# An 8-byte tile made 1024 bytes wide, in a two-layer transformer kernel in split float32

## The chip, the cores and the metric

The kernel runs on one core of one Trainium2 chip. The metric is the device time of one execution in microseconds (us); with one core it is that core's time. The inputs lie in HBM, all 16 of them in float32.

## The reference

Two layers on 256 tokens of width 2048. The first is a stick-breaking attention, the second a sparse attention in three branches (compressed, selected, window); each is followed by an MLP with a squared ReLU. Cut to what the change lies in:

```python
D_MODEL, SEQ, D_FF = 2048, 256, 8192
def sqrelu_mlp(h, w1, w2):
    return jnp.square(jax.nn.relu(h @ w1)) @ w2
...
for layer in range(2):
    if layer == 0: h = h + stick_breaking_attention(rms_norm(h, sb_norm_g[0]), ...)
    else:          h = h + native_sparse_attention(rms_norm(h, nsa_norm_g[0]), ...)
    h = h + sqrelu_mlp(rms_norm(h, mlp_norm_g[layer]), mlp_w1[layer], mlp_w2[layer])
```

## The kernel before

Each weight is read from HBM once and split into two numbers of the chip's rounded float32 type: hi = rounded(w), written by ScalarE (ACT) at line 142, and lo = w - hi, written by VectorE (DVE) at line 144. The activations are split as well (xhi and xlo in one tile xs; yhi and ylo). A product is three matmuls: hi with hi, hi with lo, lo with hi.

The unit of work is a chunk: 512 KB of weights (256 rows by 512 columns, or 512 by 256), loaded by a DMA of the SP queue into one of five buffers `raw`; in the MLPs every sixth load goes into `raw6` instead. Four hi and four lo buffers follow. TensorE (PE) uses a chunk in one of three ways:

- `chunk_T` (matmuls at line 206, 24 of them, 256 columns each): the weights are the stationary operand, the activations xs the moving one. It makes the transposed product, for `h @ w1`.
- `chunk_N` (line 173, 12 matmuls of 512 columns): the activations are stationary, the weights move, for the products with `w2` and others.
- `chunk_S` (line 269, 21 matmuls of 256 columns): the same product in the manner of Strassen, with 7 block products in place of 8. Four of the seven need sums of weight blocks, which DVE writes into a tile `ts` and which are split into hi and lo; the other three use weight blocks as they are, split into tiles `shi` and `slo`. The stationary operands are parts of yhi and ylo and of `ss`, sums of activation blocks.

`mlp` works through the 8192 hidden columns in four pieces (fg 0 to 3). For each, `group1` makes 2048 hidden columns in four blocks of 8 chunk_T; from the second piece on, a chunk_S for the previous piece's product is put in after the third and the sixth chunk_T of every block. `group2` then multiplies by `w2`: 16 chunk_N (24 in the last piece), with 8 chunk_S put between them. Per MLP that makes 24 chunk_S in group1 and 32 in group2. The order is that in which the code is written; each engine runs its instructions in that order and waits on semaphores.

Where tiles lie. The pools are laid out one behind the other, each tile of a pool behind the one before it in blocks of 32 bytes, and the code shifts some operands on purpose. The names used below: P is 128, `far` and the offsets `FAR` move a tile's start by 16 floats, 64 bytes.

```python
PAD, FAR = 64, 16
def far(pool, n, name, dtype=F32R, bufs=1):
    return pool.tile([P, n + PAD], dtype, name=name, bufs=bufs)[:, FAR:FAR + n]
...
o = (FAR, FAR) if ahi is yhi else (0, 0)          # chunk_N: where hi and lo begin in their buffers
hi, lo = ... load_split(..., o=o, gap=PAD - FAR if turn else 0)
...
W = NB // 2                                        # chunk_S
hi, lo = [wsum.tile([P, 3 * W], F32R, tag=n, name=n, bufs=1) for n in ("shi", "slo")]
```

With `turn`, the second half of a chunk's lo begins 192 bytes further on than it else would. `mlp` sets it for each chunk_N that stands before a chunk_S, and for a piece's last chunk_N. In the built program, a row of SBUF being counted in bytes from its partition's start, the operands' starts are these, modulo 256:

| operand | before | after |
|---|---|---|
| xs (moving at line 206) | 128 | 128 |
| hi, lo as weights of line 206 | 192 | 192 |
| hi, lo moving at line 173 in the MLPs | 192 | 192 |
| second half of a turned lo there | 128 | 128 |
| yhi, ylo, ss as weights of lines 173 and 269 | 192 | 192 |
| hi, lo of the sums, moving at line 269 | 128 | 128 |
| shi, slo, moving at line 269 | 160 | 128 |
| raw6, pre, uv, sq, sums, ts (ACT, DVE and DMA only) | 160 | 128 |
| raw | 128 | 128 |

Of the kernel before, what the change touches and what calls it, by code (L numbers as in the profile page):

```python
# [8 lines left out]
F32 = mybir.dt.float32  # L9
# [6 lines left out]
P = 128  # L16
T = 256
NT = T // P
# [23 lines left out]
def hybrid_kernel(  # L42
# [23 lines left out]
    def far(pool, n, name, dtype=F32R, bufs=1):  # L66
        return pool.tile([P, n + PAD], dtype, name=name, bufs=bufs)[:, FAR:FAR + n]
# [97 lines left out]
    def bank(pool, tag):  # L165
        return pool.tile([P, NB], F32, tag=tag, name=tag)
# [49 lines left out]
    def proj_T(ps, src, n0, nk=KC, then={}):  # L216

        for i in range(KD // nk):
            k0 = i * nk
            chunk_T(ps, src, k0, n0, k0 == 0, k0 + nk == KD, nk)  # L220
            if i in then:
                then[i]()
# [57 lines left out]
    def banks_S(pool, tag):  # L280

        W = NB // 2
        bs = [bank(pool, tag) for _ in range(4)]
        half = lambda j, i: bs[j][:, i * W:(i + 1) * W]
        return bs, [half(0, 0), half(1, 0), half(1, 1), half(2, 0), half(2, 1), half(3, 1), half(3, 0)]

    def add_S(nb, bs, ps, pool, scale):

        W = NB // 2
        uv = pool.tile([P, 4, W], F32, tag="pre", name="uv", bufs=1)  # L290
        u, v = uv[:, :2, :], uv[:, 2:, :]
        hb = [h[:, t, nb * NB:(nb + 1) * NB] for t in range(NT)]
        nc.scalar.activation(u[:, 0, :], ps[0], AF.Copy)
        nc.vector.tensor_tensor(v[:, 0, :], ps[5], u[:, 0, :], op=OP.add)
        nc.vector.tensor_tensor(u[:, 1, :], ps[4], v[:, 0, :], op=OP.add)
        nc.vector.tensor_tensor(v[:, 1, :], ps[6], v[:, 0, :], op=OP.add)
        f0, f1 = scale[:, 0:1], scale[:, 1:2]
        add = lambda o, x, f: nc.vector.scalar_tensor_tensor(o, x, f, o, op0=OP.mult, op1=OP.add)
        add(hb[0], bs[1], f0)
        add(hb[1], bs[2], f1)  # L300
        add(hb[0], u.rearrange("p a n -> p (a n)"), f0)
        add(hb[1].rearrange("p (a n) -> p a n", a=2), v[:, 1, :].unsqueeze(1).to_broadcast([P, 2, W]), f1)
# [8 lines left out]
    def split_evac(hi, lo, src, scale=None):  # L311

        if scale is None:
            nc.scalar.activation(hi, src, AF.Copy)  # L314
            nc.vector.tensor_tensor(lo, src, hi.bitcast(F32), op=OP.subtract)  # L315
        else:
            nc.scalar.activation(hi, src, AF.Copy, scale=scale)
            nc.vector.scalar_tensor_tensor(
                lo, src, scale, hi.bitcast(F32), op0=OP.mult, op1=OP.subtract
            )  # L320
# [44 lines left out]
    def make_rstd(layer):  # L365
        s = small.tile([P, NT], F32, tag="ms", name="ms")
        nc.vector.tensor_reduce(s, ssq_t[layer], axis=AX.X, op=OP.add)
        nc.vector.tensor_scalar(s, s, 1.0 / D, EPS, op0=OP.mult, op1=OP.add)
        r = small.tile([P, NT], F32, tag="rstd", name="rstd")
        nc.gpsimd.tensor_tensor(r, s, neghalf[:, :NT], op=OP.pow)  # L370
        return r
# [8 lines left out]
    def add_h(nb, ps, scale=None):  # L380
        for t in range(NT):
            hb = h[:, t, nb * NB:(nb + 1) * NB]
            if scale is None:
                nc.vector.tensor_tensor(hb, ps[t], hb, op=OP.add)
            else:
                nc.vector.scalar_tensor_tensor(hb, ps[t], scale[:, t:t + 1], hb, op0=OP.mult, op1=OP.add)

    def add_out(nb, ps, ov, scale):

        for t in range(NT):  # L390
            for i in range(2):
                w = NB // 2
                c = slice(nb * NB + i * w, nb * NB + (i + 1) * w)
                nc.vector.scalar_tensor_tensor(
                    h[:, t, c], ps[t][:, i * w:(i + 1) * w], scale[:, t:t + 1], h[:, t, c], op0=OP.mult, op1=OP.add
                )
                (nc.sync, nc.scalar)[i].dma_start(ov[:, t, c], h[:, t, c])
# [19 lines left out]
    def mlp(l, layer, junk, done, last=None):  # L417
        w1, w2 = mlp_w1[l], mlp_w2[l]
        ss = far(junk, KD * 4 * P, "ss").rearrange("p (a k i n) -> p a k i n", a=2, k=KD // 2, i=4)
        factor = junk.tile([P, NT], F32, name="factor", bufs=1)  # L420

        def factors():
            yield
            r = make_rstd(layer)
            nc.vector.tensor_tensor(factor, r, r, op=OP.mult)

        def in_S(fg, nb):

            for i in range(NK):
                if i == 0:  # L430
                    bs, s = banks_S(att, "att")
                chunk_S(s, w2, fg * KD + i * KC, nb * NB, i == 0, i == NK - 1, yhi, ylo, ss[:, 0], ss[:, 1],
                        koff=fg * KD)
                if i == NK - 1:
                    add_S(nb, bs, s, junk, factor)
                yield

        def group1(fg, beside_w1):

            step = lambda: next(beside_w1)  # L440
            for fb in range(D // NB):
                ps = [bank(acc, "acc") for _ in range(NB // P // 2)]
                proj_T(ps, w1, fg * D + fb * NB, then={2: step, 5: step} if beside_w1 else {})
                k, n = fb * (NB // P), NB // P
                a = junk.tile([P, n, T], F32, tag="pre", name="pre", bufs=1)
                for j in range(0, n, 2):
                    nc.scalar.activation(a[:, j:j + 2, :], ps[j // 2].rearrange("p (m t) -> p m t", m=2), AF.Relu)
                s = junk.tile([P, n, T], F32, tag="sq", name="sq", bufs=1)
                nc.scalar.activation(s, a, AF.Square)
                nc.scalar.activation(yhi[:, k:k + n, :], s, AF.Copy)  # L450
                nc.vector.tensor_tensor(ylo[:, k:k + n, :], s, yhi[:, k:k + n, :].bitcast(F32), op=OP.subtract)

                sv = s.rearrange("p (j kk) t -> p j kk t", kk=2)
                a1, a2 = [[sv[:, :, kk, t * P:(t + 1) * P] for kk in (1, 0)] for t in range(NT)]
                q = junk.tile([P, 2, 4, P], F32, tag="sums", name="sums", bufs=1)
                nc.vector.scalar_tensor_tensor(q[:, :, 0, :], a2[0], -1.0, a2[1], op0=OP.mult, op1=OP.subtract)
                nc.vector.tensor_tensor(q[:, :, 2, :], a1[0], a2[0], op=OP.subtract)
                nc.vector.tensor_tensor(q[:, :, 1, :], a2[1], q[:, :, 2, :], op=OP.subtract)
                nc.vector.tensor_tensor(q[:, :, 3, :], a1[1], q[:, :, 1, :], op=OP.subtract)
                split_evac(ss[:, 0, k // 2:k // 2 + 2], ss[:, 1, k // 2:k // 2 + 2], q)  # L460

        def group2(fg, end):

            blocks = (0, 1, 3) if end else (0, 1)
            side, si = in_S(fg, 2), 0
            for j in range(len(blocks) * NK):
                nb, i = blocks[j // NK], j % NK
                if i == 0:
                    ps = [bank(acc, "acc") for _ in range(NT)]
                out = last is not None and end and nb == 3  # L470
                aside = si < NK and j >= 4 + (1.75 if end else 1.4) * si
                chunk_N(ps, w2, fg * KD + i * KC, nb * NB, i == 0, i == NK - (2 if out else 1), yhi, ylo,
                        koff=fg * KD, by_token=out and i == NK - 1,
                        turn=aside or (not end and j == len(blocks) * NK - 1))
                if i == NK - 1:
                    if out:
                        add_out(nb, ps, last, factor)
                        return
                    add_h(nb, ps, factor)
                    if end and nb == 3:  # L480
                        done(nb, (att, "att"))
                if aside:
                    next(side)
                    si += 1
                    if si == NK and end:
                        for n in range(3):
                            done(n, (att, "att"))

        spawn(factors(), 1)
        NK = KD // KC  # L490
        for fg in range(DFF // D):
            group1(fg, in_S(fg - 1, 3) if fg else None)
            group2(fg, fg == DFF // D - 1)


    with tc.tile_pool(name="sbp", bufs=2) as sp:
# [77 lines left out]
        factor = []  # L574
# [547 lines left out]
```

## Time and profile before

| | |
|---|---|
| median of 3 runs | 2173.13 us (2172.14 to 2173.88) |
| profiled execution, its time | 2172.32 us |
| its span, first to last instruction | 2170.6 us |
| PE busy, matmuls | 2163.3 us, 14894 instructions |
| DVE busy | 1569.7 us |
| ACT busy | 1235.9 us |
| read from HBM | 401.83 MB, 186 GB/s over the span |
| MLP of layer 0, of layer 1 | about 400 to 1070 us, about 1482 us to the end |

In rows of the profile L206 is line 206 of the kernel; `acc<-xs,hi` says what an instruction writes and reads; x696 is a count. In the chain of work that ended last, a piece is a start (us from the span's start), a duration and what ran. In a window's row each engine has its busy time and its count, then come the granted TensorE clock, the share of the DMA engines and GB/s. In a row of a group the numbers behind the count are the busy time in us and the mean of one in ns, and behind the bar the idle time before it with what ended it.

### The profile page before, as it was taken

The numbers are of one execution on the slowest core, as the hardware profiler recorded it, in microseconds if no ns is written. First come the engines' busy times: TensorE is split into PE (matmuls) and PEld (weight loads), VectorE is DVE, ScalarE is ACT, GpSimd is POOL, SyncE is SP. The second block draws the span as 40 slices with busy tenths as digits, with TensorE's granted clock in tenths as the row PEclk, the third lists the DMA queues.
The fourth block names the chain that finished last, engine by engine and source line by source line (L and its number), as shares of the span: only waits on it lengthen the run. The fifth ranks groups of instructions, "written<-read, shape, count | busy, mean of one in ns | idle before, by whom it ended". The sixth has DMA issues, their size and how long they took to land.

```text
span 2170.6 us, 37272 instructions
## 1 busy us (share of the span) xinstructions
PE 2163.3 (100%) x14894; PEld 2000.6 (92%) x14894; DVE 1569.7 (72%) x2131; ACT 1235.9 (57%) x1653; POOL 45.2 (2%) x75
## 2 busy tenths in 40 slices
PE   9999999999999999999999999999999999999999
PEld 9999988998998999999898888889989989989998
DVE  5555555567778778778776887755777787787786
ACT  6555565565555555555555666655555555555553
POOL 0000000000000000000000011000000000000000
PEclk9999999999999999999999999999999999999999
DMA  7655556665656665665667554456566556656664
GB/s 243 206 164 182 168 169 192 187 198 183 208 185 201 197 191 183 208 195 185 193 186 217 165 146 141 141 177 191 185 197 211 176 194 204 194 184 204 193 193 148
DMA packets 260789, 406.34 MB, mean 187 GB/s; under 512 B 13188, under 2 KB 91912, under 8 KB 260616
## 3 DMA queue, kind: packets, MB, share of 16 engines
q1 hardware_dynamic: 259800, 403.52, 59.9%
q8 instruction: 116, 1.90, 0.3%
q14 instruction: 57, 0.47, 0.1%
q10 hardware_dynamic: 816, 0.46, 0.1%
HBM read 401.83 MB, written 2.10 MB: 186 GB/s over the span
## 4 chain that ended last, share of the span: by engine, by line
PE 98%; DVE 1%; DMA 0%; ACT 0%; issue 0%; POOL 0%; SPq 0%; DVEq 0%; ACTq 0%; POOLq 0%
PE acc L206 43%; PE acc L173 36%; PE att L269 13%; PE att L173 1%; PE att L944 1%; PE att L328 1%; DMA raw<-in_nsa_w_in_dram 0%; DVE lo L144 0%; PE att L655 0%; PE att L607 0%; PE att L882 0%; PE att L938 0%; PE att L884 0%; PE att L883 0%; PE att L936 0%; PE att L937 0%
## 5 line engine op out<-in xcount | busy, mean ns | idle before, releaser
L142 ACT ACTIVATE hi<-raw 128x1024 fp32r<-128x1024 f32 x639 | 676.4, 1060 | 616.7 <-PE acc L206 320.4
L144 DVE TENSOR_TENSOR lo<-raw,hi 128x1024 fp32r<-128x1024 f32 x639 | 777.7, 1222 | 294.4 <-ACT hi L142 282.9
L206 PE MATMUL acc<-xs,hi 128*128 128x256 f32 x5360 | 677.5, 279 | 0.0
L206 PEld LDWEIGHTS acc<-xs,hi 128*128 128x128 f32 x5360 | 646.0, 188 | 1.0
L206 PE MATMUL acc<-xs,lo 128*128 128x256 f32 x2680 | 365.4, 279 | 0.0
L206 PEld LDWEIGHTS acc<-xs,lo 128*128 128x128 f32 x2680 | 335.1, 189 | 0.0
L173 PE MATMUL acc<-hi,yhi 128*128 128x512 f32 x828 | 324.0, 391 | 0.0
L173 PE MATMUL acc<-hi,ylo 128*128 128x512 f32 x828 | 322.6, 390 | 0.0
L173 PE MATMUL acc<-lo,yhi 128*128 128x512 f32 x828 | 224.2, 392 | 0.0
L142 ACT ACTIVATE hi<-ts 128x1024 fp32r<-128x1024 f32 x112 | 118.9, 1061 | 141.0 <-PE acc L173 82.3
L173 PEld LDWEIGHTS acc<-lo,yhi 128*128 128x128 f32 x828 | 154.6, 188 | 31.7
L173 PEld LDWEIGHTS acc<-hi,ylo 128*128 128x128 f32 x828 | 155.5, 188 | 29.3 <-DVE ylo L315 0.2
L173 PEld LDWEIGHTS acc<-hi,yhi 128*128 128x128 f32 x828 | 155.5, 188 | 29.0 <-ACT yhi L314 0.2
L173 PE MATMUL acc<-hi,xs 128*128 128x512 f32 x704 | 177.2, 392 | 0.0
L245 DVE TENSOR_TENSOR ts<-raw 128x512 f32<-128x512 f32 x112 | 77.4, 691 | 131.2 <-DMA raw<-in_mlp_w_dram 130.9
L173 PEld LDWEIGHTS acc<-hi,xs 128*128 128x128 f32 x704 | 130.2, 188 | 26.3
L144 DVE TENSOR_TENSOR lo<-ts,hi 128x1024 fp32r<-128x1024 f32 x112 | 136.5, 1219 | 5.7 <-ACT hi L142 5.7
L247 ACT ACTIVATE shi<-raw 128x768 fp32r<-128x768 f32 x112 | 95.0, 848 | 55.9 <-PE att L269 39.5
L250 DVE TENSOR_TENSOR slo<-raw,shi 128x768 fp32r<-128x768 f32 x112 | 106.9, 954 | 16.6 <-PE att L269 16.4
L269 PE MATMUL att<-hi,ss 128*128 128x256 f32 x672 | 97.3, 281 | 0.0
L173 PE MATMUL acc<-lo,xs 128*128 128x512 f32 x352 | 97.1, 396 | 0.0
L269 PEld LDWEIGHTS att<-hi,ss 128*128 128x128 f32 x672 | 86.6, 188 | 0.0
(248 smaller groups left out, 2128.3 us busy)
## 6 DMA issues: line engine op xcount, KB each, us to landing
raw<-in_mlp_w_dram SPq DMA_DIRECT2D x512, 512.0 KB, 4.2
raw<-in_sb_w_qkv_dram SPq DMA_DIRECT2D x95, 512.0 KB, 3.9
raw<-in_nsa_w_in_dram SPq DMA_DIRECT2D x50, 512.0 KB, 3.7
raw<-in_sb_w_out_dram SPq DMA_DIRECT2D x32, 512.0 KB, 3.8
raw<-in_nsa_w_in_dram SPq DMA_DIRECT2D x64, 256.0 KB, 4.0
raw<-in_nsa_w_out_dram SPq DMA_DIRECT2D x32, 512.0 KB, 3.6
w1t<-in_nsa_cmp_w_dram SPq DMA_DIRECT2D x8, 512.0 KB, 4.1
h<-in_x_dram SPq DMA_DIRECT2D x8, 256.0 KB, 4.7
```

What stands on the lines that cost most here:

```text
L142: nc.scalar.activation(hi, raw, AF.Copy)
L144: nc.vector.tensor_tensor(lo, raw, hi.bitcast(F32), op=OP.subtract)
L173: mm = lambda a, b, k, t, s, e: nc.tensor.matmul(ps[t], a[:, k, t * P:(t + 1) * P], b, start=s, stop=e)
L206: nc.tensor.matmul(o, w, x[:, k0 + kk, :], start=s, stop=e, skip_group_check=True)
L245: nc.vector.tensor_tensor(ts[:, :2, :], flat[:, W:3 * W].rearrange("p (a n) -> p a n", a=2), b12, op=OP.subtract)
L247: nc.scalar.activation(hi, flat[:, :3 * W], AF.Copy)
L250: nc.vector.tensor_tensor(lo, flat[:, :3 * W], hi.bitcast(F32), op=OP.subtract)
L269: nc.tensor.matmul(ps[i], a, w, start=s, stop=e, skip_group_check=True)
L328: nc.tensor.transpose(ps[:, j * T + t * P:j * T + (t + 1) * P], h[:, t, (kp + j) * P:(kp + j + 1) * P], ident)
L944: nc.tensor.transpose(ptp[:w, j * P:(j + 1) * P], src(j), ident)
```

## The change

The tile `factor` (two floats for each partition: the square of the norm's factor for the two token tiles) is allocated with 256 floats, of which the first two are used. It is the second tile of the MLPs' pool, behind `ss`. Before, it took 32 bytes in each partition, after, 1024; all tiles of the pool behind it begin 992 bytes later. Nothing else differs: each engine has the same instructions in the same order.

```diff
         ss = far(junk, KD * 4 * P, "ss").rearrange("p (a k i n) -> p a k i n", a=2, k=KD // 2, i=4)
-        factor = junk.tile([P, NT], F32, name="factor", bufs=1)
+        factor = junk.tile([P, T], F32, name="factor", bufs=1)[:, :NT]
```

## The prediction

> **What bounds the kernel now.** I read the page first, then the waits of TensorE (PE), then the chain of work that ended last piece by piece, then windows over single lines, and at a few boundaries the timeline.
>
> ```profile
> span 2170.6 us, 37272 instructions
> PE 2163.3 (100%) x14894; PEld 2000.6 (92%) x14894; DVE 1569.7 (72%) x2131; ACT 1235.9 (57%) x1653; POOL 45.2 (2%) x75
> PEclk9999999999999999999999999999999999999999
> ```
> ```profile
> PE att L515 <- POOL ident masks.py:199: 1.6, 1, 1.6
> PE acc L534 <- ACT hi L527: 0.8, 1, 0.8
> PE att L789 <- DVE hs L784: 0.5, 1, 0.5
> PE att L836 <- DVE kc L831: 0.4, 1, 0.4
> ```
>
> PE is busy all the time at the full granted clock, and these four are all of its listed waits: 3.3 us, none of them in an MLP. So no DMA, ACT or DVE row of the MLPs is worth anything by itself; the kernel gets faster only if PE's own stream of matmuls runs denser. "Busy" does not tell how dense it is, because matmuls overlap. The pace, the time from one matmul's start to the next one's, has to be taken from the chain, whose pieces give a duration and a count. In the chain's longest pieces and around the first MLP's second group:
>
> ```profile
> 357.40 16.38 PE acc L173 x72
> 400.58 78.90 PE acc L206 x696
> 564.58 14.13 PE acc L206 x120
> 1472.47 5.66 PE acc L206 x48
> 1478.56 2.74 PE acc L206 x24
> 1481.74 78.90 PE acc L206 x696
> 1099.95 27.33 PE acc L206 x232
> ...
> 711.22 2.48 PE att L269 x21
> 716.43 8.17 PE acc L206 x72
> 724.61 2.48 PE att L269 x21
> 727.08 8.48 PE acc L206 x72
> 738.04 14.13 PE acc L206 x120
> ```
>
> The reader is to see two paces of one and the same instruction, the 128x256 matmul of line 206. Piece 400.58: 78.90/696 = 113.4 ns. Piece 564.58: 14.13/120 = 117.8 ns. In the second half of the list the switch is caught in the act: three chunks of line 206 run 8.17/72 = 113.5 ns, then comes one chunk of line 269 (the Strassen-like chunk_S), and the next three run 8.48/72 = 117.8 ns, and so on to the group's end. The chunk_S itself runs 2.48/21 = 118.1 ns. It is no matter of the clock, and no wait stands between:
>
> ```profile
> 440.00:470.00 30.00, 30.00 (x267) 30.00 (x266) 1.00 0.63 196
> 593.00:605.00 12.00, 12.00 (x104) 12.00 (x104) 1.00 0.58 197
> ```
>
> Both windows over line 206 show PE busy throughout and clock 1.00, the first before any chunk_S, the second between two of them.
>
> So the pace is something that the stream keeps until it is tipped over. What tips it over I read by laying the addresses of the built program beside the trace. At line 206 the moving operand (xs) begins at 128 modulo 256 and the weights at 192, at both paces. In chunk_S the weights (yhi, ylo, ss) are at 192 too, the moving hi and lo at 128, but the moving shi and slo at 160. Nine of its 21 matmuls stand at that other distance, and the fast stream does not come back after the first of them. Twice more the trace shows that a foreign distance sets the pace: piece 1472.47 comes straight from 128x512 matmuls with moving operand and weights both at 192 and runs slow (5.66/48 = 117.9), until four transposes end it (1478.56 reads 114 ns, 1481.74 is fast); piece 1099.95 follows two transposes with weights at 64 and is slow for all its 232 matmuls.
>
> **The change, part by part.** No instruction is added, removed or moved: each engine's order is the same. What changes is where nine tiles lie, raw6, pre, uv, sq, sums, both ts, shi and slo: from 160 to 128 modulo 256.
>
> *ACT, DVE.* Their cost at the two places can be read now, since raw lies at 128 and ts at 160:
>
> ```profile
> L142 ACT ACTIVATE hi<-raw 128x1024 fp32r<-128x1024 f32 x639 | 676.4, 1060 | 616.7 <-PE acc L206 320.4
> L144 DVE TENSOR_TENSOR lo<-raw,hi 128x1024 fp32r<-128x1024 f32 x639 | 777.7, 1222 | 294.4 <-ACT hi L142 282.9
> L142 ACT ACTIVATE hi<-ts 128x1024 fp32r<-128x1024 f32 x112 | 118.9, 1061 | 141.0 <-PE acc L173 82.3
> L144 DVE TENSOR_TENSOR lo<-ts,hi 128x1024 fp32r<-128x1024 f32 x112 | 136.5, 1219 | 5.7 <-ACT hi L142 5.7
> ```
>
> 1060 against 1061 ns and 1222 against 1219: nothing. *DMA.* One load in six goes to raw6. The trace has it under raw's name, so its landing can't be told apart; it lies behind ACT, which idles 320 us for PE at line 142, that is, the loads run ahead. I take zero for it; were it dearer or cheaper, the same cover would hide it.
>
> *PE in group1.* After the change all 21 matmuls of chunk_S have the distance of line 206 (moving 128, weights 192). I take it that the quick pace then goes on through chunk_S and behind it, as it goes on through 696 matmuls at 400.58 that change weights, banks and moving tile all the time. chunk_S: 2.48 - 21 x 0.1134 = 0.10 us, and group1 has 8 of them in 3 of 4 groups of 2 layers: 48 x 0.10 = 4.8 us. Line 206 behind them: of a group's 32 chunks the first three are fast already, 29 chunks x 24 matmuls x 6 groups = 4176 x (117.8 - 113.4 = 4.4 ns) = 18.4 us. Bounds for this term: 0 if the pace doesn't hold, 18.4 if it does everywhere; I take the upper one, since of the rows above every stretch that keeps the distance keeps its pace.
>
> *PE in group2.* Here chunk_S stands between chunks of line 173, moving and weights both at 192. Going in and coming out in the quick pace have their own prices, which two boundaries show:
>
> ```profile
> 715.35 1.08 PE L173 MATMUL acc<-lo,yhi 128*128 128x512 f32 x4
> 716.27 1.99 PE L206 MATMUL acc<-xs,hi 128*128 128x256 f32 x16
> 718.10 1.07 PE L206 MATMUL acc<-xs,lo 128*128 128x256 f32 x8
> 719.00 1.98 PE L206 MATMUL acc<-xs,hi 128*128 128x256 f32 x16
> 720.82 1.07 PE L206 MATMUL acc<-xs,lo 128*128 128x256 f32 x8
> ...
> 1560.47 0.39 PE L173 MATMUL acc<-hi,yhi 128*128 128x512 f32 x1
> 1560.71 0.40 PE L173 MATMUL acc<-hi,ylo 128*128 128x512 f32 x1
> 1560.94 0.39 PE L173 MATMUL acc<-hi,yhi 128*128 128x512 f32 x1
> 1561.17 0.39 PE L173 MATMUL acc<-hi,ylo 128*128 128x512 f32 x1
> ```
>
> At 715.35 a "turned" chunk, whose last two matmuls read lo at 128, precedes line 206: the first sixteen take 716.27 to 718.10 = 1.83 us, the later sixteen 719.00 to 720.82 = 1.82. In: 0.01 us. The same turn stands before every chunk_S of group2. At 1560.47 the fast line 206 is left for 192: the first three steps take 0.70 us, 0.233 each, where 16.38/72 = 0.2275 is usual. Out: 0.02 us. Left over: 0.10 - 0.03 = 0.07 us x 64 chunks = 4.5 us. Bounds: 0 and 6.4 (no price in or out).
>
> *Given back.* Six groups now end fast and pay 0.02 each: 0.1 us. DVE has to keep up:
>
> ```profile
> 826.00:887.00 61.00, 61.00 (x353) 53.88 (x351) 51.49 (x68) 35.11 (x37) 0.00 (x0) 1.00 0.59 188
> 887.00:998.00 111.00, 111.00 (x936) 110.52 (x935) 83.36 (x102) 61.31 (x66) 0.00 (x0) 1.00 0.64 199
> GB/s 243 206 164 182 168 169 192 187 198 183 208 185 201 197 191 183 208 195 185 193 186 217 165 146 141 141 177 191 185 197 211 176 194 204 194 184 204 193 193 148
> ```
>
> In a group2 (826 to 887) it is busy 51.49 of 61 us, in a group1 83.36 of 111, so there is cover; should it fail here and there, slo is what PE would wait for first, in group2 with its 4.5 us at stake. DMA at 199 GB/s in group1 would have to deliver 4% more, 207; it moved 243 in the first slice.
>
> *Sum.* 4.8 + 18.4 + 4.5 - 0.1 = 27.6 us. The profiled execution took 2172.3 us, so 2144.7; the median of the runs is 0.8 above that execution, 2145.5.
>
> A rule speaks against all this. The Trainium skill, "SBUF — State Buffer", section "Who interferes with whom", gives PE two read ports, one for the moving operand and one for the weights, independent of each other, and says that PE never waits on anyone. By it, moving shi and slo changes nothing on PE and the sum is 0. The rows at 716.43 and 727.08 are hard to square with it.
>
> **The rivals.**
> 1. *Nothing changes.* Operand addresses don't set the pace, something else in chunk_S does (its change of weight tiles, its half-bank outputs). For it: in chunk_S even the matmuls with moving operands at 128 run slow, so the distance alone is not enough. Against: the same distance holds the fast pace for 78.90 us twice. Time: 2172.3 + 0.8 = 2173. This is where the page's rule would end as well.
> 2. *Only group1 gains.* The 512-column chunks of group2 don't settle within three steps after a fast chunk_S, or DVE is late with slo. 2145.5 + 4.5 = 2150.
> 3. *The quick pace breaks now and then.* A single upset costs the rest of a group: if half of line 206 stays slow, 2145.5 + 9.2 = 2154.7. For it: two transposes did as much at 1099.95. Against: nothing but chunk_S stands within a group1.
> 4. *Slower.* chunk_S now leaves the stream so that line 173 in group2 doesn't recover, so that all its matmuls run at the 0.233 us of 1560.47 instead of 0.2275: 144 chunks x 12 x 0.006 = 10.4 us, while group1 stays slow as it is: 2173.1 + 10.4 = 2183.5. It decides from the point where line 206 gains under 10 us, that is, where over half of its chunks stay slow. Against: at 1560.47 recovery takes three steps.
>
> **How the numbers follow.** The full gain 0.76, rival 1 0.09, rival 2 0.06, rival 3 0.05, rival 4 0.04. The prediction is the full gain, 2145.5. Its own spread is small (the terms are counts times measured steps), 2141 to 2149; rivals 2 and 3 are taken in up to 2157, which leaves 0.13 outside. 0.2% of the time, 4.3 us, is about what a measurement of this kernel tells from no change: faster 0.87 (full gain, rivals 2 and 3), same 0.09, slower 0.04.
>
> **What would show it.** In the chain, pieces of line 206 in group1 from the first chunk_S on should read 113.4 ns each, 14.13 becoming 13.6 for 120, or merge into longer fast pieces; line 269 should read 2.38 for 21 in group1 and about 2.39 in group2; line 173 behind it about 0.02 longer per piece. Line 142 and 144 keep 1060 and 1220 ns. The prediction is wrong if the pieces of line 206 behind the first chunk_S still read 117.8, or if PE shows waits for slo or DMA in the MLPs that weren't there.

## The result and the profile after

The changed kernel takes 2147.66 us (median of 4 runs, 2144.79 to 2148.14), the one before 2172.82 beside it: a ratio of 0.9881, 95% interval 0.9864 to 0.9898. The profiled execution took 2144.79 us, 27.5 less than the profiled one before.

From the page of the changed kernel (span, busy time of each engine, granted TensorE clock in tenths):

```profile
span 2143.1 us, 37272 instructions
PE 2136.4 (100%) x14894; PEld 1973.4 (92%) x14894; DVE 1563.9 (73%) x2131; ACT 1231.6 (57%) x1653; POOL 45.2 (2%) x75
...
PEclk9999999999999999999999999999999999999999
```

PE is as full as before, with as many instructions and the same clock; the 27 us are gone from its busy time. Where they went shows the chain of work that ended last, in the stretch of the first MLP that was read before (start, duration, what ran):

```profile
706.86 2.39 PE att L269 x21
709.25 2.75 PE acc L173 x12
712.00 8.18 PE acc L206 x72
720.17 2.38 PE att L269 x21
722.55 8.16 PE acc L206 x72
730.71 2.38 PE att L269 x21
733.09 13.60 PE acc L206 x120
```

Behind the first chunk_S (line 269, piece 720.17) line 206 now reads 8.16/72 = 113.3 ns and 13.60/120 = 113.3 ns, where it was 117.8. chunk_S reads 2.38 in group1 and 2.39 in group2, where it was 2.48. Line 173 behind a chunk_S reads 2.75, where it was 2.73 (below, from the chain before): the price of leaving.

```profile
713.70 2.73 PE acc L173 x12
```

The six group1 that hold chunk_S have 4554 steps from one matmul of line 206 to the next. After the change 10 of them are slow (116 to 122 ns), all of them the first one or two behind a turned chunk; before, 4139 were.

### The profile page after: what moved, and what is told of

The parts are those of the page before. It is cut to its first block, busy times and chain, and to the rows that moved or that the text cites. A ratio compares the mean times of both kernels' runs of the same rounds, so it can differ in the third digit from the quotient of the medians.

```text
span 2143.1 us, 37272 instructions
## 1 busy us (share of the span) xinstructions
PE 2136.4 (100%) x14894; PEld 1973.4 (92%) x14894; DVE 1563.9 (73%) x2131; ACT 1231.6 (57%) x1653; POOL 45.2 (2%) x75
## 4 chain that ended last, share of the span: by engine, by line
PE 98%; DVE 1%; DMA 0%; ACT 0%; issue 0%; POOL 0%; SPq 0%; DVEq 0%; ACTq 0%; POOLq 0%
PE acc L206 43%; PE acc L173 37%; PE att L269 12%; PE att L173 1%; PE att L328 1%; PE att L944 1%; DMA raw<-in_nsa_w_in_dram 0%; DVE lo L144 0%; PE att L655 0%; PE att L607 0%; PE att L882 0%; PE att L938 0%; PE att L884 0%; PE att L883 0%; PE att L936 0%; PE att L937 0%
## 5 line engine op out<-in xcount | busy, mean ns | idle before, releaser
L142 ACT ACTIVATE hi<-raw 128x1024 fp32r<-128x1024 f32 x639 | 676.0, 1060 | 576.1 <-PE acc L206 274.0
L206 PE MATMUL acc<-xs,hi 128*128 128x256 f32 x5360 | 665.2, 277 | 0.0
L206 PEld LDWEIGHTS acc<-xs,hi 128*128 128x128 f32 x5360 | 634.4, 188 | 0.9
L206 PE MATMUL acc<-xs,lo 128*128 128x256 f32 x2680 | 359.3, 277 | 0.0
L206 PEld LDWEIGHTS acc<-xs,lo 128*128 128x128 f32 x2680 | 329.2, 188 | 0.0
L142 ACT ACTIVATE hi<-ts 128x1024 fp32r<-128x1024 f32 x112 | 118.7, 1060 | 136.8 <-PE acc L173 67.8
L144 DVE TENSOR_TENSOR lo<-ts,hi 128x1024 fp32r<-128x1024 f32 x112 | 136.5, 1219 | 3.5 <-ACT hi L142 3.5
```

Source lines behind the costliest of these rows:

```text
L142: nc.scalar.activation(hi, raw, AF.Copy)
L144: nc.vector.tensor_tensor(lo, raw, hi.bitcast(F32), op=OP.subtract)
L206: nc.tensor.matmul(o, w, x[:, k0 + kk, :], start=s, stop=e, skip_group_check=True)
```

## The experiments

One theory and three rivals stood at the start. The *distance theory*: PE's pace hangs on where the moving operand begins relative to the weights, modulo 256; a foreign distance tips the stream of matmuls over, and it stays slow. The rivals: other moved tiles carry the gain; each matmul pays for itself alone; the absolute place counts.

**Which tile.** In the first kernel shi and slo alone are moved, in the second all others.

```diff
 # e1, on the kernel before
+        wsum.tile([P, 56], F32, tag="gap", name="gap", bufs=1)
         hi, lo = [wsum.tile([P, 3 * W], F32R, tag=n, name=n, bufs=1) for n in ("shi", "slo")]
 # e2, on the kernel after
+        wsum.tile([P, 8], F32, tag="gap", name="gap", bufs=1)
         hi, lo = [wsum.tile([P, 3 * W], F32R, tag=n, name=n, bufs=1) for n in ("shi", "slo")]
```

> The tile factor has its 8 bytes again and an unused tile of 224 bytes stands ahead of shi, so shi and slo alone begin at 128 modulo 256; raw6, pre, uv, sq, sums and ts stay at 160. Distance theory (PE's pace hangs on the distance of moving operand and weights, and only shi and slo are read by PE): the whole gain, 2147 to 2149 us, 113.4 ns at line 206 throughout the MLPs. Rival (the loads into raw6, or ACT and DVE on the other tiles, carry a part): clearly above 2150, up to 2173.

Measured: 2148.75 us, ratio 0.9886 (0.9872 to 0.9901), line 206 at 113.3 ns in the MLPs (chunk_S stands at line 270 in this kernel and the next):

```profile
724.08 2.38 PE att L270 x21
726.46 8.16 PE acc L206 x72
```

> As after the change, but an unused tile of 32 bytes ahead of shi puts shi and slo back to 160; all others stay at 128. Distance theory: no gain at all, 2171 to 2174 us, line 206 at 117.8 ns behind the first chunk_S of a group. Rival (other tiles carry it): near 2148, or in between.

Measured: 2173.46 us, ratio 1.0004 (0.9995 to 1.0013). The chain in e2 around the first chunk_S of a group1:

```profile
718.88 8.17 PE acc L206 x72
727.05 2.48 PE att L270 x21
729.53 8.48 PE acc L206 x72
```

So shi and slo carry the whole change, and raw6, ts and the rest nothing that can be measured.

**Does one foreign matmul carry on to the next?**

```diff
-        hi, lo = [wsum.tile([P, 3 * W], F32R, tag=n, name=n, bufs=1) for n in ("shi", "slo")]
+        hi = wsum.tile([P, 3 * W], F32R, tag="shi", name="shi", bufs=1)
+        wsum.tile([P, 8], F32, tag="gap", name="gap", bufs=1)
+        lo = wsum.tile([P, 3 * W], F32R, tag="slo", name="slo", bufs=1)
```

> As after the change, but slo alone at 160; shi stays at 128. If one matmul at a foreign distance tips the stream over for good: in group1 the first slo matmul does it, line 206 and the chunk_S there stay at 117.8 ns, and only group2 keeps the 14 matmuls ahead of slo, 64 x 14 x 4.4 ns less 0.01 each = 3.3 us: about 2169.5. Rival (each matmul pays for its own operand's place, nothing is passed on): the three slo matmuls of nine keep their old pace, so about two thirds of the gain stay, 2156.

Measured: 2169.37 us, ratio 0.9985 (0.9975 to 0.9994). The chain (chunk_S at line 271):

```profile
713.24 2.73 PE acc L173 x12
715.97 8.17 PE acc L206 x72
724.15 2.41 PE att L271 x21
726.56 8.48 PE acc L206 x72
735.04 2.48 PE att L271 x21
737.51 14.13 PE acc L206 x120
```

The first chunk_S of a group1 enters quick and takes 2.41: its first 14 matmuls are quick, and the first slo matmul tips it over. From there everything is slow, the next chunk_S too (2.48), although its six shi matmuls lie right. Three matmuls of 21 cost most of the gain: 2169.37 us against 2147.66. That each matmul pays only for itself is refuted.

**Does the way in count?**

```diff
-                        turn=aside or (not end and j == len(blocks) * NK - 1))
+                        turn=False)
```

> As after the change, but no chunk_N of the MLPs is turned: all of its moving lo begins at 192, and what follows (chunk_S, or line 206 of the next piece) is entered straight from 192. If the pace depends on how a stream is entered: it runs slow as at 1472.47 in the profile before, chunk_S and line 206 of all groups but each MLP's first at 117.8 ns; the gain is lost and the first three chunks of six groups with it (6 x 72 x 4.4 ns = 1.9 us), less what the turns cost (70 x 0.013 = 0.9): about 2174. Rival (the distance alone sets the pace): 0.9 less than after the change, about 2147.

Measured: 2172.61 us, ratio 1.0000 (0.9990 to 1.0009), 1.4 us below the 2174 that was summed.

```profile
713.95 2.72 PE acc L173 x12
716.66 8.48 PE acc L206 x72
725.14 2.47 PE att L269 x21
727.62 8.48 PE acc L206 x72
```

Here the operands of chunk_S and of line 206 lie as after the change, and line 206 is slow from its first chunk on (8.48). The right distance allows the quick pace; it doesn't make it. The stream has to be brought there, which the two turned matmuls do.

**Other places, and all tiles moved together.** The unused tile ahead of shi gets 16, 32 or 48 floats in place of 8 of e2; e8 has a tile of 8 floats at the head of the first pool:

```diff
+    cpool.tile([P, 8], F32, name="first")
     h = cpool.tile([P, NT, D], F32, name="h")
```

> As after the change, but an unused tile of 64 bytes ahead of shi puts shi and slo to 192 modulo 256, the very place of their weights. If the stream is tipped over by any distance but the one it runs at (64 below the weights): hi at 128 behind shi at 192 is entered as line 206 is from 192 without a turn, so 117.8 ns in chunk_S and behind it in group1, 2171 to 2175 us. Rival (only starts that are no multiple of 64 do harm, 160 among them): near 2147.7, as after.

> As after the change, but an unused tile of 128 bytes ahead of shi puts shi and slo to 0 modulo 256. If the pattern repeats every 256 bytes, this is a foreign distance and tips the stream over: 2171 to 2175 us. Rival (it repeats every 128 bytes, or every 64): near 2147.7.

> As after the change, but an unused tile of 192 bytes ahead of shi puts shi and slo to 64 modulo 256, 128 below the weights. Distance theory: a foreign distance, 2171 to 2175 us. Rival (repeats every 64): near 2147.7.

> As after the change, but an unused tile of 32 bytes at the head of the first pool moves every tile of the kernel up by 32 bytes: shi, slo, xs, hi and lo moving begin at 160, the weights of lines 206 and 269 at 224. If the distance between moving operand and weights is what counts, nothing changes: 2145 to 2150 us, 113.4 ns at line 206. Rival (the absolute place, 128 good and 160 bad): line 206 is slow in the MLPs and before them, 2173 or more.

Measured: e8 2146.92 us, ratio 0.9881 (0.9852 to 0.9909), with the paces of after (lines below; in this kernel the lines are one further): shi at 160 is quick when its weights are at 224. So 160 by itself isn't the cause.

```profile
722.31 2.38 PE att L270 x21
724.69 8.16 PE acc L207 x72
```

But the other three missed both expectations: 2153.73 (192), 2152.00 (0) and 2155.53 us (64). The chain with 64, the dearest:

```profile
714.14 8.17 PE acc L206 x72
722.32 2.48 PE att L270 x21
724.79 8.16 PE acc L206 x72
732.96 2.48 PE att L270 x21
735.43 13.60 PE acc L206 x120
```

chunk_S is as dear as before the change (2.48; 2.44 and 2.43 with 192 and 0), but line 206 behind it is quick at once. So a foreign distance has two prices: one on the spot, 4 to 8 us in all by the medians of two runs each, most of it in chunk_S, and one that is passed on, 18.4 us, which at these three places isn't asked. The theory was too strong.

Nor does the place of an operand alone decide what is passed on. With shi at 0, the ninth to eleventh matmul of chunk_S, which read hi at 128, take 114.2, 113.3 and 113.4 ns in group1, where chunk_S follows line 206. In group2, where it follows line 173, the same three take 117.5, and the quick pace comes back only over the last three matmuls. And the distance 0, from which the stream comes back here (shi at 192), is the one that line 173 handed on to line 206 in e4. Where the stream comes from counts as well.

**Is it the 32?** 160 is no whole number of 64 bytes from the weights, 0, 64 and 192 are. Two more such places (24 and 56 floats in the unused tile):

> As after the change, but an unused tile of 96 bytes ahead of shi puts shi and slo to 224 modulo 256, 32 above the weights. The starts 0, 64 and 192 made chunk_S itself dearer (2.43 to 2.48 us), but line 206 behind it came back to 113.4 ns. If what keeps it from coming back is a distance that is no whole number of 64 bytes: 117.8 ns behind the first chunk_S, 2169 to 2175 us. Rival (160 is alone in this): 2150 to 2156.

> As after the change, but an unused tile of 224 bytes ahead of shi puts shi and slo to 96 modulo 256, 96 below the weights. If a distance that is no whole number of 64 bytes keeps line 206 from coming back: 2169 to 2175 us. Rival (160 is alone in this): 2150 to 2156.

Measured: 2151.37 us, ratio 0.9900 (0.9880 to 0.9920), and 2151.85, ratio 0.9902 (0.9883 to 0.9922). The chain with 224:

```profile
712.93 8.17 PE acc L206 x72
721.10 2.45 PE att L270 x21
723.55 8.16 PE acc L206 x72
```

The rival holds: of the seven places tried, 160 alone leaves line 206 slow. Within chunk_S the steps at 224, averaged over all 112 chunk_S, show the way back: 118.6, 120.2, 115.0, 113.9 and 113.4 ns at the seventh to eleventh matmul, where hi at 128 follows. At 160 the same five stay at 116.7 to 118.3. What makes 160 different was not found; 32, the eighth multiple of 32, was not tried.

**Another place in the kernel.** The piece of 232 slow matmuls behind the transposes of line 377, whose weights begin at 64:

```diff
-    small.tile([P, 48], F32, name="gap", bufs=1)
+    small.tile([P, 64], F32, name="gap", bufs=1)
...
+    small.tile([P, 48], F32, name="gap2", bufs=1)
     with tc.tile_pool(name="m1p", bufs=2) as mp:
```

> As after the change, but the factors rstd that the two transposes of line 377 take as weights begin at 128 modulo 256 in place of 64 (the unused tile gap has 64 floats instead of 48, and 48 floats more lie at the pool's end, so the pools behind begin where they did, modulo 256). If it is the place of these weights that leaves the 232 matmuls of line 206 behind them slow: that piece reads 26.3 us instead of 27.3, 1.0 us less in all, which the profile shows and the times hardly. Rival (another cause, such as that these weights are one number read 128 times): 27.3 as before.

Measured: 2144.49 us (2143.75 to 2145.26), ratio 0.9870 (0.9853 to 0.9886). The chain of after, then that of this kernel:

```profile
1086.38 0.22 PE att L377 x2
1086.60 27.33 PE acc L206 x232
```
```profile
1086.16 0.22 PE att L377 x2
1086.38 26.32 PE acc L206 x232
```

1.01 us, as worked out. Two transposes with weights at 128 and 132 in place of 64 and 68 leave the stream quick. The other tiles of that pool moved by 64 bytes too; line 206 reads none of them. Here the moving operand of the transposes stays at 128 and only the weights move; in e1 and e2 the moving operands moved under weights that stay at 192. So the weights' start counts as well as the moving operand's. This kernel has the lowest median of those run.

**What the median lacks.** After the change three of four runs took 2147.6 to 2148.1 and the profiled one 2144.8. The profile of e1, taken at 2148.97 us, lists a PE wait in its MLPs that the profile after doesn't (waiting, waited for: us, times, longest):

```profile
PE att L270 <- DVE slo L251: 3.3, 4, 1.3
```

Behind it, from 485 to 720 us (the first two group2 and the group1 between), DVE and ACT wait longer in e1, the first fence, than after the change, the second:

```profile
DVE ts L245 <- DMA raw<-in_mlp_w_dram: 46.2, 16, 4.8
...
ACT ss L315 <- DVE sums L460: 16.0, 4, 5.6
ACT shi L248 <- DVE slo L251: 11.7, 7, 2.7
```
```profile
DVE ts L245 <- DMA raw<-in_mlp_w_dram: 36.6, 16, 3.9
...
ACT ss L314 <- DVE sums L459: 11.4, 4, 3.5
...
ACT shi L247 <- DVE slo L250: 4.4, 4, 1.3
```

DVE stands before a chunk_S's load, then writes slo late, and PE waits. Between the two traces PE falls 4.2 us behind, nearly all of it in the first MLP's first two group2 (3.8) and the second MLP's first (0.5).

PE's steps say more than the list of waits. The steps to a chunk_S's first two slo matmuls (the 15th and 16th of its 21) are longer than the quick pace by 0.3 us in all in the profile after, 4.7 in e1, 2.7 in e8 and 0.5 in e9. Without this the spans are 2142.8, 2142.6, 2142.9 and, with the 1.0 of its transposes added, 2142.5 us. So among these four profiled executions the spread is the wait for slo.

The last kernel gives DVE more room there:

```diff
-                aside = si < NK and j >= 4 + (1.75 if end else 1.4) * si
+                aside = si < NK and j >= 4 + (1.75 if end else 1.55) * si
```

> As after the change, but in group2 of each MLP's first three pieces the eight chunk_S are spread wider among the 16 chunk_N (one per 1.55 chunk_N in place of 1.4, so that the last stands behind the last chunk_N). The same work, DVE with more time between two chunk_S. If the spread of the runs after the change (2144.8 to 2148.1) is PE waiting for slo in the first group2: the wait goes, 2144 to 2146 us with a spread under 1.5, and no PE wait for slo in the profile. Rival (the spread comes from elsewhere, or the loads are late whatever the spacing): 2145 to 2149 as after.

Measured: 2145.30 us (2144.48 to 2146.49), ratio 0.9873 (0.9857 to 0.9890); the profile lists no wait for slo, and the steps to slo are 0.5 us longer in all. That is the first expectation, but for a spread of 2.0. That the spacing did it isn't shown: e9, with the old spacing, took 2143.75 to 2145.26, with its 1.0 added 2144.8 to 2146.3, which is no slower. The three runs after the change that took 2147.6 to 2148.1 weren't profiled; that their 2 to 3 us are this wait is likely, not shown.

## Why the prediction was right, point by point

- *PE's pace, not its waits, is what the time hangs on.* Right: of PE's listed waits one shrank, from 0.8 to 0.2 us, and PE's busy time fell by 26.9 us. The list leaves small waits out: in the MLPs, where the text saw none, the steps to slo were 0.3 us longer in all before the change too.
- *ACT and DVE cost the same at 128 as at 160; the loads into raw6 are hidden.* Right: 1060 and 1219 ns after for ts at 128, and e1 has the gain with raw6 at 160, e2 loses it with raw6 at 128.
- *chunk_S in group1 0.10 us each, line 206 behind it 4.4 ns per matmul.* Right: 2.48 to 2.38, 117.8 to 113.3 ns. e3 and e4 show the two things that the term took for granted: that the stream carries its pace on, and that it has to come in quick.
- *group2 0.07 us each, with 0.01 in and 0.02 out.* Right: 2.39 and 2.75 where 0.09 less and 0.02 more were summed.
- *The sum, 27.6 us.* The two profiled executions differ by 27.5, the medians by 25.2. The missing 2.3 are most likely the term that was set at zero, "DVE has to keep up": PE's wait before slo was 0.3 us in the profile after and 4.7 in that of e1. The text named slo in group2 as what PE would wait for first and then took the cover for whole; a listed wait for slo was also one of its signs of being wrong, and e1's profile has one. Busy shares such as 51.49 of 61 us didn't show that DVE stands there before a load and has its work bunched behind it.
- *Rival 1 and the page's rule.* The Trainium skill's two independent read ports of PE ("SBUF — State Buffer", "Who interferes with whom") don't fit e1 and e2 as the prediction read them: moving two tiles by 32 bytes changes the time by 24 to 26 us, and PE's pace with it, while the engines that write them keep their times (shi a median of 847 to 849 ns, slo 952 to 953, in all four kernels). Why the two operands bear on each other is not shown.
- *What was read from one place too widely:* that any foreign distance tips the stream over. It forecast this change rightly, since 160 is the place at hand, but e5, e6, e7, e10 and e11 refute it as a rule. The sum didn't need the rule: that line 206 is slow behind shi and slo at 160, and quick in stretches at the new distance, was read from the trace.

## What to carry to other kernels

An engine that is busy throughout can still run at two paces: divide the pieces of the chain by their counts, form by form, before taking PE's work as fixed. Where the same matmul has two paces, lay operand starts modulo 256 beside the point at which the pace switches, and look at the neighbours: the cause may lie many matmuls earlier. And where PE is made denser, look at the waits of the engine that feeds it in its tightest stretch, not at its busy share.

## What the runs showed of the hardware that was not expected

- PE's pace hung on where moving operand and weights begin: 113.3 or 117.8 ns for the same 128x256 matmul, clock 1.00, no wait. shi and slo at 160 were slow with weights at 192 (2173.5 us, e2) and quick with weights at 224, when all tiles were moved by 32 bytes (2146.9).
- The pace is handed on from matmul to matmul, over more than a hundred of them. Three foreign matmuls of every 21 in chunk_S kept line 206 slow, up to 120 matmuls to the next chunk_S (2169.4 against 2147.7 us); two transposes kept 232 slow.
- Of seven distances of shi and slo one is free (2147.7), five cost 4 to 8 us on the spot and line 206 behind chunk_S is quick again, and one, 32 bytes below the weights, is passed on (2172.8). Why that one, stays open; and how soon the stream recovers hangs on how it came in, as the two paces behind shi at 0 show.
